# When a tile's transposing transfer and its merge are asked for in the last group of a decoder layer's first up-projection

## The chip, the cores and the metric

The kernel runs on one core of one Trainium2 chip. The metric is the device time of one execution in microseconds (us); lower is better. All inputs and outputs are float32.

## What is computed

The reference is one decoder layer over 256 positions of width 2048: a conditioned SwiGLU feed-forward part, a gated pair of token mixers, a second SwiGLU part and a final norm. The change lies in the first feed-forward part, `x + 0.5 * gate * SwiGLU1(h)`:

```
mod = (c_act @ w_ada[l] + b_ada[l]).reshape(b, N_MOD, D_MODEL)
h = modulate(rms_norm(x, norm_ffn1[l]), mod[:, 0], mod[:, 1])
x = x + 0.5 * mod[:, 2][:, None, :] * swiglu(h, w_ffn1_gu[l], w_ffn1_down[l])
...
def swiglu(h, w_gu, w_down):
    gate, up = jnp.split(h @ w_gu, 2, axis=-1)
    return (jax.nn.silu(gate) * up) @ w_down
```

`w_gu` is 2048 x 11264 and `w_down` 5632 x 2048. The product of silu(gate) and up has positions on its rows; the down-projection needs it turned, with positions on its columns.

## The kernel before

**Products.** Every product of full width is made of three: weights and activations are split in a high part (rounded to fp32r) and the rest, and `products` (L354 to L369) issues high x high, low x high and high x low on TensorE, for each of two tiles of 128 positions. A load of weights, 1 MB, goes through SP's DMA queue into one of four `raw` buffers. ScalarE casts it to the high part `wh` in two halves (L375), VectorE makes the rest `wl` (L377), and each half feeds 12 matmuls of 128x512. The pool of `wh` and `wl` has three buffers, so ScalarE can be almost three halves ahead of TensorE.

**The first up-projection.** Its first 16 half chunks of 512 columns (n = 0 to 15; even n a gate, odd n an up) are worked in four groups of the contraction, so that work can start before the whole of h is there. The loop stands at L1233. In the last group (`final`) each of the 16 visits takes one load of four blocks, so 24 matmuls. A visit n runs `visit` (its matmuls), then `ready` (the load of the next visit, and the cast of that load's first half), then `turn_step`, and behind an odd n `swiglu_up`, which adds the sums of the earlier groups, takes silu(gate) x up for the two tiles and leaves them to be turned. In this group only, `swiglu_up` is given `behind` (the last cast), so that silu comes behind it on ScalarE. Visits 0 to 7 also do passes of the conditioning (`tick`), which load rows of `w_ada` into the same four `raw` buffers.

**Turning a tile.** For n = 1, 3, 5, 7, 9 and 11 the two tiles are turned by DMA, in three steps each (L525): `apart` copies the tile into two planes of 16-bit words (ScalarE, two copies at L535, into one of three `flat` buffers); `turn` issues a transposing transfer on SP (L540) from `flat` to one of four `back` buffers; `together` merges the planes at the tile's place (ScalarE, two copies at L551). For n = 13 and 15 TensorE turns the tiles (L518). The lines that decide what a step waits for:

```
flat = ctx.enter_context(tc.tile_pool(name="flat", bufs=3))
back = ctx.enter_context(tc.tile_pool(name="back", bufs=4))
...
            with tc.issue_after(cast[-1]):
                for i in range(2):
                    nc.scalar.copy(planes[:, i, :], words(src)[:, :, i])
...
            turned = back.tile([P, 2, KB, P], U16, tag="back", name=nm("back"))
            nc.sync.dma_start_transpose(
...
            with tc.issue_after(cast[-1]):
                for i in range(2):
                    nc.scalar.copy(into[:, :, :, i], held["turned"][:, i])
```

**What sets the order.** SP's order is that of the program (`manual_schedule`, L103): an instruction that waits on SP holds all behind it. On the other engines a scheduler sets the order when the kernel is built; `issue_after(cast[-1])` keeps the copies of a step behind the latest cast that was issued when the step was reached. Since `ready` comes before `turn_step` in a visit, that is the cast of the first half of the next visit's load. `later` (L651) is the list of steps that a chunk's two tiles take, one a visit: in it, `a0, a1` are the plane copies of the two tiles, `t0, t1` the transposing transfers and `m0, m1` the merges. A chunk that ends at visit n does a0 at n+2, a1 at n+3, t0 at n+7, t1 at n+8 and both merges at n+10, so what n = 7 to 11 leave goes on among the gemm parts of `ffn_up` (L722), which follows the group and whose `turn_step` is at L444.

Of the kernel before, what the change touches and what calls it, by code (L numbers as in the profile page):

```python
# [77 lines left out]
def layer_kernel(  # L78
# [42 lines left out]
    def nm(s):  # L121
        uid[0] += 1
        return f"{s}_{uid[0]}"
# [10 lines left out]
    def t512():  # L134
        return tmp.tile([P, CH], F32, tag="t512", name=nm("t"))
# [188 lines left out]
    turns = []  # L324
# [189 lines left out]
    def transpose_to(dest, src_of, n, ps=None):  # L514

        ps = ps or bank()
        for j in range(n):
            nc.tensor.transpose(ps[:, j * P : (j + 1) * P], src_of(j), ident)  # L518
        nc.any.tensor_copy(dest, ps[:, : n * P])
# [5 lines left out]
    def turn_by_dma(dest, src, pool=flat, tag="flat"):  # L525


        held = {}

        def apart():  # L530
            planes = pool.tile([P, CH], F32, tag=tag, name=nm("flat"))
            planes = planes.bitcast(U16).rearrange("p (i n) -> p i n", i=2)
# [3 lines that stand above are left out]
            held["planes"] = planes  # L536

        def turn():
            turned = back.tile([P, 2, KB, P], U16, tag="back", name=nm("back"))
            nc.sync.dma_start_transpose(  # L540
                turned.rearrange("p i k n -> p (i k) n"),
                held["planes"].rearrange("p i n -> p (i n)"),
            )
            held["turned"] = turned

        into = dest.bitcast(U16).rearrange("p k (s i) -> p k s i", i=2)

        def together():
# [4 lines that stand above are left out]
        return apart, turn, together  # L553
# [97 lines left out]
    def later(work, then=None, quick=False):  # L651

        (a0, t0, m0), (a1, t1, m1) = work
        order = [a0, a1, None, None, None, t0, t1, None, m0]
        for f in order[:7] + order[7 + quick :]:
            yield
            if f is not None:
                f()
        m1()
        if then is not None:  # L660
            then()

    def later_by_pairs(work):

        for apart, _, _ in work:
            apart()
        for _ in range(5):
            yield
        for a in range(0, len(work), 2):
            for which in (1, 2):  # L670
                yield
                for parts in work[a : a + 2]:
                    parts[which]()
# [21 lines left out]
    def swiglu_up(banks_g, banks_u, tiles, ci, parts=None, by_dma=False, behind=None):  # L695

        k0 = ci * KB
        dest = tiles[k0 // KD].rearrange("p (k s) -> p k s", s=S)
        kk = k0 % KD
        work = []  # L700
        for t in range(NT):
            s = t512()
            g, u = banks_g[t], banks_u[t]
            if parts is not None:
                nc.vector.tensor_add(s, g, parts[0][t])
                nc.vector.tensor_add(parts[1][t], u, parts[1][t])
                g, u = s, parts[1][t]
            with nullcontext() if behind is None else tc.issue_after(behind):
                nc.scalar.activation(s, g, AF.Silu)
            nc.vector.tensor_mul(s, s, u)  # L710
            if by_dma:
                work.append(turn_by_dma(dest[:, kk : kk + KB, t * P : (t + 1) * P], s))
                continue
            transpose_to(
                dest[:, kk : kk + KB, t * P : (t + 1) * P],
                lambda j: s[:, j * P : (j + 1) * P],
                KB,
            )
        if work:
            turns.append(later(work))  # L720

    def ffn_up(held, w, tiles, first, bg=None, turned=(), ahead=None):  # L722
        for ci in range(first, DFF // CH):
            bg = bg or gemm(held, w, [ci * CH])[0]
            bu = gemm(held, w, [DFF + ci * CH], ahead=ahead)[0]
            swiglu_up(bg, bu, tiles, ci, by_dma=ci in turned)
            bg = ahead = None
# [240 lines left out]
    behind = [[back.tile([P, CH], F32, tag="back", name=nm("back")) for _ in range(NT)] for _ in range(2)]  # L968
# [264 lines left out]
    for g, ks in enumerate(groups):  # L1233
# [11 lines left out]
        for i, n in enumerate(order):  # L1245
# [31 lines left out]
            if not final:  # L1277
                to_parts(n)
            elif n % 2:
                swiglu_up(  # L1280
                    banks.pop(n - 1),
                    banks.pop(n),
                    tiles,
                    n // 2,
                    (part_of(n - 1), part_of(n)),
                    n // 2 < 6,
                    cast[-1],
                )
# [40 lines left out]
    work = []  # L1329
# [153 lines left out]
    for ci in range(4):  # L1483
        b = in_chunk(O_SQ + ci * CH)
        work = []
# [16 lines left out]
    for a, off in ((0, O_RQ), (1, O_RK)):  # L1502
        for ci in range(2):
            b = in_chunk(off + ci * CH)
            work = []
# [93 lines left out]
    for ci in range(4):  # L1599
        b = in_chunk(O_RG + ci * CH)  # L1600
        work = []
# [11 lines left out]
    for p in range(2):  # L1613
        sg = first if p == 0 else gates(p)
        c0s = [(2 * p + i) * CH for i in range(2)]
        for g, a, w in ((1, a_swa, w_swa_branch), (0, a_ret, w_ret_branch)):
            assert g == 1 or not turns
            banks = gemm(a, w[0], c0s)
            for i in range(2):
                for t in range(NT):  # L1620
                    nc.vector.tensor_mul(sg[:, g, i, t, :], sg[:, g, i, t, :], banks[i][t])
        work = []
        for i in range(2):
            for t in range(NT):
                m = sg[:, 0, i, t, :]
                nc.vector.tensor_add(m, m, sg[:, 1, i, t, :])
                k0 = (2 * p + i) * KB
                dest = mt[:, k0 : k0 + KB, t * P : (t + 1) * P]
                if p == 0 or i == 1:
                    work.append(turn_by_dma(dest, m, tmp, "t512"))  # L1630
                    continue
                transpose_to(dest, lambda j: m[:, j * P : (j + 1) * P], KB)
        soon(later_by_pairs(work) if p == 0 else later_at_once(work))
# [135 lines left out]
```

## Time and profile before

| what | before |
|---|---|
| median of 3 runs | 2367.28 us |
| the three runs | 2367.73, 2367.28, 2357.96 us |
| the profiled execution's own time | 2357.64 us |
| its span, from first to last instruction | 2355.5 us |
| mean granted TensorE clock | 0.999 |
| TensorE busy | 2335.7 us, 99% |
| VectorE busy | 1673.1 us, 71% |
| ScalarE busy | 1367.2 us, 58% |
| the last group of the first up-projection | about 289 to 377 us of the span |

Profiled times count from the start of the span. The profiled execution's own time holds 2.14 us more than the span, which lie around it. A DMA's row on SP is the time in which SP issues it; its landing is told apart, from issue to the last byte. Where a row says x2 or x4, its time runs from the first of them to the end of the last.

### The profile page before, as it was taken

Reading aid. Unit: us, or ns where it says so; the run is one execution under the profiler, and the core shown is the slowest. Engines: PE = TensorE matmul, PEld = TensorE weight load, DVE = VectorE, ACT = ScalarE, POOL = GpSimd, SP = SyncE. Lnnn points to the kernel's source line nnn. Section 1 sums busy time; section 2 is a strip of 40 time slices with the busy share of each in tenths; the row PEclk is TensorE's granted clock in tenths of the full one; section 3 lists DMA queues with packets and bytes.
Section 4 is the critical chain, followed back from the end, with each engine's and each line's share of the span. In section 5 each row is a group of like instructions: output and inputs, shape, how many; then the busy total and the mean of one; then the engine's idle time right before and its main releaser. Section 6 shows DMA issues by size and latency. Waiting matters only on the chain.

```text
span 2355.5 us, 28357 instructions
## 1 busy us (share of the span) xinstructions
PE 2335.7 (99%) x10445; PEld 1918.6 (81%) x10445; DVE 1673.1 (71%) x2576; ACT 1367.2 (58%) x1888; POOL 18.3 (1%) x27
## 2 busy tenths in 40 slices
PE   8999999999999999999999999999999999999998
PEld 5888888888888888778888888888888888888887
DVE  7788888778867768976777776676555555555656
ACT  6766567455556567774556564465455454455544
POOL 0000000000000000000000000000000000000000
PEclk9999999999999999999999999999999999999999
DMA  9989889988765889876778787754767768666553
GB/s 383 375 323 361 355 294 328 336 306 293 302 237 220 293 267 255 258 212 254 267 273 306 288 310 281 272 204 179 259 237 256 242 239 268 223 231 202 193 197 125
DMA packets 191901, 630.24 MB, mean 268 GB/s; under 512 B 113105, under 2 KB 114769, under 8 KB 121233
## 3 DMA queue, kind: packets, MB, share of 16 engines
q1 hardware_dynamic: 189266, 617.41, 74.6%
q0 software_dynamic: 1600, 9.83, 1.0%
q8 instruction: 82, 1.34, 0.2%
q10 hardware_dynamic: 896, 1.19, 0.1%
q14 instruction: 57, 0.47, 0.1%
HBM read 598.47 MB, written 4.22 MB: 256 GB/s over the span
## 4 chain that ended last, share of the span: by engine, by line
PE 96%; DMA 2%; DVE 1%; ACT 1%; issue 0%; SPq 0%; DVEq 0%; ACTq 0%
PE pa L360 93%; DMA raw<-in_w_ffn_gu_dram 1%; DMA rows_x<-in_w_ada_dram 1%; PE ps L1453 0%; DVE slot L220 0%; PE pd L1369 0%; DVE wl L377 0%; ACT wh L375 0%; DMA x_sb<-in_x_dram 0%; PE ps L360 0%; PE pa L1099 0%; PE ps L895 0%; PE pd L1099 0%; DVE rows_x L220 0%; PE ps L1369 0%
## 5 line engine op out<-in xcount | busy, mean ns | idle before, releaser
L377 DVE TENSOR_TENSOR wl<-raw,wh 128x1024 fp32r<-128x1024 f32 x792 | 963.5, 1225 | 511.0 <-ACT wh L375 451.6
L375 ACT CAST wh<-raw 128x1024 fp32r<-128x1024 f32 x792 | 830.6, 1054 | 818.7 <-PE pa L360 752.6
L360 PE MATMUL pa<-wh,hh 128*128 128x512 f32 x2184 | 597.0, 391 | 3.0 <-ACT wh L375 1.7
L360 PE MATMUL pa<-wh,hl 128*128 128x512 f32 x2184 | 592.6, 389 | 0.0
L360 PE MATMUL pa<-wl,hh 128*128 128x512 f32 x2184 | 586.2, 390 | 0.2
L360 PEld LDWEIGHTS pa<-wh,hh 128*128 128x128 f32 x2184 | 407.5, 188 | 91.6 <-ACT wh L375 2.9
L360 PEld LDWEIGHTS pa<-wl,hh 128*128 128x128 f32 x2184 | 409.4, 188 | 86.7 <-DVE wl L377 1.0
L360 PEld LDWEIGHTS pa<-wh,hl 128*128 128x128 f32 x2184 | 409.8, 188 | 86.1 <-issue 0.4
L360 PE MATMUL pa<-wh,a 128*128 128x512 f32 x1824 | 452.1, 389 | 0.0
L360 PEld LDWEIGHTS pa<-wh,a 128*128 128x128 f32 x1824 | 341.7, 188 | 70.6
L360 PE MATMUL pa<-wl,a 128*128 128x512 f32 x912 | 245.1, 389 | 0.0
L220 DVE CUSTOM_DVE_ANT_0 slot<-slot,cact 128x512 f32<-128x512 f32 (+2 forms) x288 | 219.3, 812 | 30.0 <-DMA slot<-in_w_ada_dram 29.5
L360 PEld LDWEIGHTS pa<-wl,a 128*128 128x128 f32 x912 | 171.1, 188 | 35.4
L551 ACT COPY slot<-back 128x512 uint16<-128x512 uint16 x148 | 98.7, 766 | 0.0
L220 DVE CUSTOM_DVE_ANT_0 rows_x<-rows_x,cact 128x512 f32<-128x512 f32 x124 | 78.7, 686 | 18.0 <-DMA rows_x<-in_w_ada_dram 17.8
L410 ACT CAST a<-slot 128x512 fp32r<-128x512 f32 x114 | 70.6, 620 | 29.3 <-PE pa L360 29.0
L535 ACT COPY flat<-t 128x512 uint16<-128x512 uint16 x136 | 76.7, 617 | 8.9 <-DVE t L1526 5.7
L411 DVE TENSOR_TENSOR a<-slot,a 128x512 fp32r<-128x512 f32 x114 | 77.8, 684 | 0.3 <-ACT a L410 0.3
L220 DVE CUSTOM_DVE_ANT_0 raw<-raw,cact 128x512 f32<-128x512 f32 (+1 forms) x92 | 60.7, 709 | 14.6 <-DMA raw<-in_w_ada_dram 14.5
L1219 ACT COPY slot<-pa 128x512 f32<-128x512 f32 x72 | 38.6, 589 | 21.2 <-PE pa L360 21.0
L360 PE MATMUL pa<-wh,home 128*128 128x512 f32 x160 | 39.5, 389 | 0.0
L220 DVE DVE_READ_ACCUMULATOR2_ANT sums<- 128x1 f32 x440 | 35.9, 82 | 0.0
(232 smaller groups left out, 1087.0 us busy)
## 6 DMA issues: line engine op xcount, KB each, us to landing
raw<-in_w_ffn_gu_dram SPq DMA_DIRECT2D x160, 1024.0 KB, 5.5
raw<-in_w_in_dram SPq DMA_DIRECT2D x104, 1024.0 KB, 5.8
raw<-in_w_ffn_down_dram SPq DMA_DIRECT2D x88, 1024.0 KB, 4.9
slot<-in_w_ada_dram SPq DMA_DIRECT2D x87, 1024.0 KB, 7.4
rows_x<-in_w_ada_dram SPq DMA_DIRECT2D x31, 1024.0 KB, 7.1
raw<-in_w_ada_dram SPq DMA_DIRECT2D x22, 1024.0 KB, 5.7
raw<-in_w_swa_branch_dram SPq DMA_DIRECT2D x16, 1024.0 KB, 5.0
raw<-in_w_ret_branch_dram SPq DMA_DIRECT2D x16, 1024.0 KB, 5.4
```

Source lines behind the costliest of these rows:

```text
L220: nc.vector.tensor_tensor_reduce(out=w[:, at], in0=w[:, at], in1=cact[:, at], scale=1.0, scalar=0.0, op0=ALU.mult, op1=ALU.add, accum_out= ...
L360: product = nc.tensor.matmul(banks[t], act[:, j, t * P : (t + 1) * P], weights[:, j, :], start=starts and i == 0 and j == 0, stop=ends and ...
L375: cast.append(nc.scalar.copy(hi, src).ins)
L377: low.append(nc.vector.tensor_sub(lo, src, hi.bitcast(F32)).ins)
L410: nc.scalar.copy(hi, v)
L411: nc.vector.tensor_sub(lo, v, hi.bitcast(F32))
L535: nc.scalar.copy(planes[:, i, :], words(src)[:, :, i])
L551: nc.scalar.copy(into[:, :, :, i], held["turned"][:, i])
L1219: nc.scalar.copy(p, b)
```

## The change

In the last group, and only there, the list `later` gives way to a new one, `evenly`. With it a chunk that ends at visit n does a0 at n+2, t0 and a1 at n+3, t1 at n+4, m0 at n+7 and m1 at n+8. The number of copies and transfers is the same. The list that the chunks of `ffn_up` take stays `later`.

```diff
+    def evenly(work):
+
+        (a0, t0, m0), (a1, t1, m1) = work
+        for fs in ((), (a0,), (t0, a1), (t1,), (), (), (m0,), (m1,)):
+            for f in fs:
+                f()
+            yield
+
...
         if work:
-            turns.append(later(work))
+            turns.append((later if behind is None else evenly)(work))
```

The new function moves every later line number up by eight (L1158 is L1166, L709 is L717).

SP's queue before, in the second half of the group. A transfer names its `back` buffer and its `flat` source; a load names its `raw` buffer; 484, 493, 504, 513, 524, 533 and 546 are the loads of visits 9 to 15, and 565 the first of `ffn_up`. These rows begin behind the load of visit 9:

```order
L540 DMA_TRANSPOSE back_487_2754<-flat_437_2510 128x8x128
L1158 DMA raw_493_2789<-in_w_ffn1_gu_dram 128x2048
L540 DMA_TRANSPOSE back_496_2795<-flat_447_2561 128x8x128
L1158 DMA raw_504_2840<-in_w_ffn1_gu_dram 128x2048
L540 DMA_TRANSPOSE back_507_2846<-flat_456_2604 128x8x128
L1158 DMA raw_513_2881<-in_w_ffn1_gu_dram 128x2048
L540 DMA_TRANSPOSE back_516_2891<-flat_466_2655 128x8x128
L1158 DMA raw_524_2936<-in_w_ffn1_gu_dram 128x2048
L540 DMA_TRANSPOSE back_527_2942<-flat_477_2705 128x8x128
L1158 DMA raw_533_2977<-in_w_ffn1_gu_dram 128x2048
```

The same place now, from the load of visit 9 (488) on; 497, 508, 517, 528, 537 and 550 are the loads of visits 10 to 15:

```order
L1166 DMA raw_488_2756<-in_w_ffn1_gu_dram 128x2048
L540 DMA_TRANSPOSE back_491_2764<-flat_481_2713 128x8x128
L1166 DMA raw_497_2799<-in_w_ffn1_gu_dram 128x2048
L540 DMA_TRANSPOSE back_500_2807<-flat_492_2766 128x8x128
L1166 DMA raw_508_2852<-in_w_ffn1_gu_dram 128x2048
L540 DMA_TRANSPOSE back_511_2860<-flat_501_2809 128x8x128
L1166 DMA raw_517_2895<-in_w_ffn1_gu_dram 128x2048
L540 DMA_TRANSPOSE back_520_2903<-flat_512_2862 128x8x128
L1166 DMA raw_528_2948<-in_w_ffn1_gu_dram 128x2048
```

Before, the transfer behind the load of visit 9 is the first of the twelve; now it is the fifth, and the first four (`back_447`, `back_457`, `back_468` and `back_480`) stand behind the loads of visits 5 to 8. From the fifth on a transfer takes a `back` buffer that an earlier one had, four before it.

ScalarE before, from the cast of the first half of the load of visit 12 (513) on. The two merges free the buffers `back_487` and `back_496`, which the transfers `back_527` and `back_536` take again:

```order
L375 CAST wh_514_2883<-raw_513_2881 128x1024
L551 COPY slot_8_117<-back_487_2754 128x4x128 x2
L551 COPY slot_8_117<-back_496_2795 128x4x128 x2
L709 ACTIVATE t_518_2896<-t_518_2896 128x512
L709 ACTIVATE t_519_2901<-t_519_2901 128x512
L375 CAST wh_522_2920<-raw_513_2881 128x1024
L535 COPY flat_508_2848<-t_479_2713 128x512 x2
L375 CAST wh_525_2938<-raw_524_2936 128x1024
```

ScalarE now, from the cast of the first half of the load of visit 9 (488) on; the merges free `back_447`, `back_457` and `back_468`, which the transfers `back_491`, `back_500` and `back_511` take again:

```order
L375 CAST wh_489_2758<-raw_488_2756 128x1024
L551 COPY slot_8_117<-back_447_2561 128x4x128 x2
L535 COPY flat_492_2766<-t_460_2616 128x512 x2
L375 CAST wh_495_2783<-raw_488_2756 128x1024
L375 CAST wh_498_2801<-raw_497_2799 128x1024
L551 COPY slot_8_117<-back_457_2606 128x4x128 x2
L535 COPY flat_501_2809<-t_482_2716 128x512 x2
L717 ACTIVATE t_502_2812<-t_502_2812 128x512
L717 ACTIVATE t_503_2817<-t_503_2817 128x512
L375 CAST wh_506_2836<-raw_497_2799 128x1024
L375 CAST wh_509_2854<-raw_508_2852 128x1024
L551 COPY slot_8_117<-back_468_2659 128x4x128 x2
```

Before, two tiles were merged at every second visit; now one tile is merged at each, directly behind the first cast of a load.

## The prediction, made before the changed kernel had run

> **What bounds the kernel now.** I read the page first, for the engine that carries the span.
>
> ```profile
> span 2355.5 us, 28357 instructions
> PE 2335.7 (99%) x10445; PEld 1918.6 (81%) x10445; DVE 1673.1 (71%) x2576; ACT 1367.2 (58%) x1888; POOL 18.3 (1%) x27
> PE 96%; DMA 2%; DVE 1%; ACT 1%; issue 0%; SPq 0%; DVEq 0%; ACTq 0%
> ```
>
> TensorE (PE) is busy for 99% of the span and makes 96% of the chain that ended last. Next I read the table of stretches over the last group; its columns are the busy time (and count) of PE, PEld, DVE, ACT and POOL, the granted clock, the DMA share and GB/s.
>
> ```profile
> 299.70:321.50 21.80, 21.80 (x98) 18.06 (x97) 21.66 (x38) 14.67 (x20) 0.00 (x0) 1.00 0.78 298
> 321.50:343.20 21.70, 21.70 (x98) 17.86 (x97) 18.94 (x29) 13.71 (x20) 2.16 (x4) 1.00 1.07 327
> 343.20:365.00 21.80, 21.80 (x98) 18.06 (x97) 15.58 (x19) 17.90 (x26) 0.00 (x0) 1.00 0.67 190
> ```
>
> TensorE has no idle time in any of them: 98 matmuls in 21.8 us, or 0.222 us each, so a visit's 24 take 5.3 us. Nothing in this group can give time back. What the change can do is to make TensorE wait where it doesn't now, and a matmul that comes late there is not made up for later, since the engine is full on both sides.
>
> So the question is how early the weights are. In ScalarE's order of time (start, duration, engine, line), these rows are the first cast of the load of visit 9, and of the load after visit 15, which is the first of `ffn_up`:
>
> ```profile
> 331.83 1.05 ACT L375 CAST wh<-raw 128x1024 fp32r<-128x1024 f32 x1 [1.19 <-issue]
> 371.56 1.04 ACT L375 CAST wh<-raw 128x1024 fp32r<-128x1024 f32 x1
> ```
>
> and in TensorE's order the transposes that stand behind six matmuls of visit 15, and the first four matmuls of the visit after it:
>
> ```profile
> 371.94 0.60 PE L518 MATMUL ps<-small_c,t 128*128 128x128 f32 x4
> 376.93 1.07 PE L360 MATMUL pa<-wh,hh 128*128 128x512 f32 x4
> ```
>
> TensorE uses that weight 5.4 us after its cast began (376.93 - 371.56). A cast takes 1.05, so some 4.3 us is all the cover there is.
>
> Last I read what SP, which asks for the weights in the program's order, waits for. First the longest row of SP's waits in the stretch 290 to 400, then SP's order of time:
>
> ```profile
> SPq L540 <- ACT slot L551: 34.0, 4, 13.1
> ...
> 338.20 0.33 SPq L1158 DMA_DIRECT2D raw<-in_w_ffn_gu_dram  x1
> 350.48 1.23 SPq L540 DMA_TRANSPOSE back<-flat  x1
> 351.81 0.53 SPq L1158 DMA_DIRECT2D raw<-in_w_ffn_gu_dram  x1
> 352.43 1.23 SPq L540 DMA_TRANSPOSE back<-flat  x1
> 353.76 0.74 SPq L1158 DMA_DIRECT2D raw<-in_w_ffn_gu_dram  x1
> ```
>
> This is the stall on which all turns. The transfer at 350.48 is `back_527`, the first that takes a `back` buffer again. SP waited for the merge that frees it (longest 13.1 us), and the load behind it went out only at 351.81. A transfer that waits holds the weights. Before, TensorE survives it, because the merge it waits for stands behind the cast of visit 12's load while the load it holds is that of visit 14: the load of visit 13 was out already, at 338.20, and two transfers are freed at once.
>
> **The change part by part.** The counts stay: twelve transfers, 24 plane copies and 24 merge copies. Two of the copies at L519 move from ScalarE to VectorE; both have idle time there, so they cost nothing.
>
> *The first four transfers* move up by four visits, into buffers that are free. They wait for plane copies now. A plane copy stands behind the first cast of a load, and the transfer holds the load two visits on; a round is cast, copy, transfer, load and landing, some 9 us by the rows below (0.96 + 1.04 + 1.33 + 5.6), against 10.7 for two visits. It just fits, and I cost it at nothing; what it may take off the cover of 4.3 us is in the upper bound.
>
> *The fifth transfer and those behind it* cost the time. By the orders shown, `back_491` needs the buffer of `back_447`, whose merge stands behind the first cast of visit 9's load (488); behind `back_491` on SP stands the load of visit 10 (497). Then `back_500` needs a merge behind the first cast of that very load, and holds the load of visit 11, and so on to the load after visit 15. From here on each load can be asked for only when the load before it has landed and been cast: a round is now one visit, not two.
>
> The round's pieces, from ScalarE's order of time, with the rows of SP above:
>
> ```profile
> 348.10 1.06 ACT L375 CAST wh<-raw 128x1024 fp32r<-128x1024 f32 x1 [1.14 <-PE pa L360]
> 349.06 2.66 ACT L551 COPY slot<-back 128x512 uint16<-128x512 uint16 x4
> 351.58 1.15 ACT L709 ACTIVATE t<-t 128x512 f32<-128x512 f32 x2
> ...
> 367.05 1.13 ACT L535 COPY flat<-t 128x512 uint16<-128x512 uint16 x2
> 368.09 1.05 ACT L375 CAST wh<-raw 128x1024 fp32r<-128x1024 f32 x1
> 369.04 2.66 ACT L551 COPY slot<-back 128x512 uint16<-128x512 uint16 x4
> ```
>
> Cast to merge is 0.96 us (348.10 to 349.06), merge to transfer 1.42 (349.06 to 350.48), transfer to load 1.33 (350.48 to 351.81): together 3.71. Then the load lands, and the next cast begins. Landings, from the DMA issues (count, KB, us to landing), alone in the stretches 351.7 to 352, 364.4 to 364.6 and 338.1 to 338.4, then the min, median and max of all loads of L351 and of L1158:
>
> ```profile
> raw<-in_w_ffn_gu_dram SPq DMA_DIRECT2D x1, 1024.0 KB, 5.6
> raw<-in_w_ffn_gu_dram SPq DMA_DIRECT2D x1, 1024.0 KB, 5.2
> raw<-in_w_ffn_gu_dram SPq DMA_DIRECT2D x1, 1024.0 KB, 9.2
> ...
> DMA to landing us min/median/max: 4.6/5.0/14.1
> ...
> DMA to landing us min/median/max: 4.9/7.8/14.2
> ```
>
> The first two went out right behind a transfer, with little else in flight, as the loads of the round would: I take 5.6. The third shared the engines with the gate row and constants that GpSimd loads at that time; the load of visit 10 meets these too, so it gets 7.4, half way from 5.6 to 9.2. From landing to cast I allow 0.1.
>
> The sum runs from the cast of visit 9, which I leave at 331.83, to that of the load after visit 15, seven loads on. Six steps of 3.71 make 22.3. The seventh is longer, for two transfers stand ahead of that load, and the second waits for the merge behind the *second* cast of visit 15: cast 0.96, merge pair 1.26 (half of 349.06 to 351.58), plane copies 1.04 (367.05 to 368.09), cast 0.95, merge to transfer 1.42, transfer to load 1.33, together 7.0. Landings: 7.4 + 6 x 5.6 = 41.0, and 7 x 0.1 = 0.7. In all 22.3 + 7.0 + 41.0 + 0.7 = 71.0, so the cast begins at 402.8 and TensorE can use it at 403.9, a cast of 1.05 later. Now it does at 376.93. The loss is 27.0 us; it includes the use of the cover, which is gone after the first round or two.
>
> Bounds: with every landing at 4.6, the smallest, the landings are 32.2 and the loss 18; with every one at the median of 7.8, 54.6 and 41. Below that lies only a failure of the mechanism (a rival).
>
> Against: the silent gain. The four waits of SP, 34.0 us in all, change their place and are worth nothing where they are, as TensorE had no idle time in 299.7 to 365.
>
> Here a rule of the Trainium skill speaks differently. Its page "DMA: Bandwidth & Descriptors", section "Issuing engines are not separate DMA queues", says that who starts a DMA matters only for the issuing sequencer's time, which is usually small beside the transfer. By that the twelve transfers would cost their issue alone wherever they stand, and the sum would be zero. SP's 13.1 us ahead of 350.48 disagree: the time of the sequencer here is its wait, not its issue.
>
> On the profiled execution's own time, 2357.64 us (span 2355.5 and 2.14 around it), 27.0 make 2384.6. The runs of before lie at two levels, about 2358 (one run, and the profile) and 2367.5 (two runs, with the median of 2367.28), and no view tells me why. On the upper level it would be 2394.5. I predict the middle, 2389.
>
> **The rivals.**
>
> *The weights stay hidden (not slower).* The loads asked for ahead of the fifth transfer would carry TensorE to the end of the round. From 331.83 to 375.88, the latest start of a cast that keeps 376.93, there are 44.05 us; the issue parts and the small lags take 22.3 + 7.0 + 0.7 = 30.0, which leaves 14.05 for seven landings, 2.0 each. Hidden means landings of 2.0 us or less. The smallest row says 4.6. It could still be so if a merge came ahead of the cast. Time: as before, 2357.6 to 2367.5. Chance 0.07.
>
> *Early asking pays (not slower either).* A transfer that is asked four visits earlier has landed long before its merge, so ScalarE never waits for it and the merge comes sooner; SP would then wait less, and more loads would be ahead. For it is this row, of those who wait for the transfers in the group:
>
> ```profile
>   ACT flat L535: 2.5, 3
> ```
>
> Three times ScalarE waits 2.5 us in all for a transfer to free its `flat` buffer, and that would go. Against it: a merge is placed by the step list, not by the landing, and no wait is ended by a landing in the round above. Gain at most nothing, for want of idle time on TensorE: 2357.6 to 2367.5. Chance 0.05.
>
> The Trainium skill's page "DMA: Bandwidth & Descriptors", section "Rules for kernel authors", is of this mind: issue a DMA early, wait for it late, and its fixed cost overlaps. What it leaves open is what stands behind the early one in the same queue.
>
> *Congestion (slower still).* If the transfers' issue takes long again and the landings are long, the round grows.
>
> ```profile
> L540 SPq DMA_TRANSPOSE back<-flat x12: 1231/1234/2640, 321.8 to 383.3; - x12
> ```
>
> These are the min, median and max in ns of a transfer's issue in the group. With 2.64 in place of 1.23 for the seven issues of the sum (+9.9) and seven landings of 7.8 (54.6 in place of 41.0, +13.6) the loss is 50.5: 2408 to 2418. Against it: in the round only one load and one transfer are in flight at a time, and the rows of `w_ada` come only before visit 8. Chance 0.06.
>
> **How the numbers follow.** The forecast has 0.82; its own range, 18 to 41 us on either level, is 2375.6 to 2408.5. The two hidden cases have 0.12 and lie below 2370, congestion 0.06 above; leaving both out is within the 2 in 10, so the range is 2374 to 2407. About 0.5%, or 12 us, is what a measurement of this kernel can tell from no change. Faster by more than that has no mechanism, only the spread of the runs: 0.02. Within: the two hidden cases, 0.10 of them, and 0.03 for the low end of the forecast against an upper level of before: 0.13. Slower: 0.85.
>
> **What would show it.** In the profile after: TensorE idle in visits 10 to 15, and none before 340; its idle time ended by ScalarE's cast (L375), and the casts waiting for DMA of `raw`; SP's loads of visits 11 to 15 about 9.4 us apart, each 1.3 us behind a transfer; SP's wait for the merges (L551) in most of eight places; and from the second load of `ffn_up` on the same rate as before. The prediction is wrong if loads there go out every 5.3 us, if the gaps on TensorE are ended by something else than the casts, or if a loss of this size stands outside 340 to 405.

## The result and the profile after

| what | before | after |
|---|---|---|
| median, executions beside each other (6 and 6) | 2361.03 us | 2385.89 us |
| lowest and highest of them | 2356.32 to 2367.73 us | 2383.84 to 2387.37 us |
| the profiled execution's own time | 2357.64 us | 2386.35 us |
| its span | 2355.5 us | 2384.2 us |
| TensorE takes the first weights of `ffn_up` | 376.93 us | 404.46 us |

The kernel is slower: ratio 1.0101, 95% interval 1.0081 to 1.0121. Before lies mostly between 2355.5 and 2360 us and now and then between 2363 and 2368.5, and its six executions here hold both, so their median lies in between; in the two sets run beside the experiments its medians are 2356.92 (25 executions) and 2357.32 (17). Against these two medians, and between the two profiled executions, the loss is 28.6 to 29.0 us.

The page of after: the span, the busy time by engine, the shares of the chain that ended last, and the group of matmuls whose idle time grew (busy us, mean ns, idle us just before them and what ended most of it).

```profile
span 2384.2 us, 28354 instructions
PE 2346.1 (98%) x10445; PEld 1922.6 (81%) x10445; DVE 1675.6 (70%) x2578; ACT 1366.2 (57%) x1886; POOL 18.6 (1%) x27
PE 93%; DMA 3%; DVE 2%; ACT 1%; issue 1%; SPq 0%; DVEq 0%; ACTq 0%
L360 PE MATMUL pa<-wh,hh 128*128 128x512 f32 x2184 | 600.0, 393 | 18.4 <-ACT wh L375 17.6
```

The work is the same and TensorE still has nearly all of the chain. What moved is the idle time of one group of matmuls, 18.4 us, ended by the casts; before it was this row:

```profile
L360 PE MATMUL pa<-wh,hh 128*128 128x512 f32 x2184 | 597.0, 391 | 3.0 <-ACT wh L375 1.7
```

Where it lies shows in the table of stretches of after (the same columns as in the prediction):

```profile
321.50:343.20 21.70, 21.50 (x96) 17.35 (x94) 16.22 (x26) 10.63 (x16) 2.17 (x4) 1.00 0.91 249
343.20:365.00 21.80, 14.12 (x50) 10.13 (x51) 10.53 (x13) 11.27 (x17) 0.00 (x0) 0.92 0.48 145
365.00:387.00 22.00, 17.60 (x64) 13.26 (x62) 10.69 (x13) 13.16 (x21) 0.00 (x0) 0.85 0.52 137
387.00:409.00 22.00, 15.39 (x61) 11.37 (x60) 14.55 (x23) 13.01 (x20) 0.00 (x0) 0.85 0.69 244
409.00:431.00 22.00, 22.00 (x98) 18.21 (x97) 15.24 (x27) 13.91 (x18) 0.00 (x0) 1.00 0.98 400
```

In three stretches TensorE does 50, 64 and 61 matmuls where 21.8 us held 98 before; to 342.6 and from 409 on it is full. The DMA share falls to about a half in the middle: the transfer engines are idle half of the time just when weights are wanted. That speaks against a lack of bandwidth. The chain of waits, cut to 290 to 420, says what the time went to instead: first its head line for before, then for after pieces of it (start, duration, what), the load of visit 8, then those from the load of visit 10 on, with one round in full, and the end.

```profile
by line: PE pa L360 98.8%; PE ps L518 1.3%; PE ps L295 0.1%
```

```profile
319.72 9.79 DMA raw<-in_w_ffn_gu_dram
...
337.35 7.78 DMA raw<-in_w_ffn_gu_dram
345.23 0.37 ACT wh L375
345.83 0.36 issue
346.18 1.41 ACT slot L551 x2
347.59 1.00 ACT flat L535 x2
348.95 5.30 DMA raw<-in_w_ffn_gu_dram
...
358.06 5.20 DMA raw<-in_w_ffn_gu_dram
...
390.81 0.85 ACT wh L375
...
397.73 5.54 DMA raw<-in_w_ffn_gu_dram
403.37 1.05 ACT wh L375
404.46 15.59 PE pa L360 x58
```

The chain has no piece of TensorE from 310 to 404. From the load of visit 10 on it goes in a circle: a load, a cast, a merge, a transfer, and the next load. (At 347.59 it names plane copies, L535, where SP's order has a transfer at 347.62; more on this name below.) SP's order of time shows the circle from its side:

```profile
335.95 1.29 SPq L540 DMA_TRANSPOSE back<-flat  x1
337.35 0.52 SPq L1166 DMA_DIRECT2D raw<-in_w_ffn_gu_dram  x1
347.62 1.24 SPq L540 DMA_TRANSPOSE back<-flat  x1
348.95 0.53 SPq L1166 DMA_DIRECT2D raw<-in_w_ffn_gu_dram  x1
...
358.06 0.53 SPq L1166 DMA_DIRECT2D raw<-in_w_ffn_gu_dram  x1
...
393.19 4.48 SPq L540 DMA_TRANSPOSE back<-flat  x2
397.73 0.57 SPq L351 DMA_DIRECT2D raw<-in_w_ffn_gu_dram  x1
```

Each load of these rounds goes out 1.33 to 1.47 us behind the start of a transfer, about 0.1 behind the end of its issue, and loads are 9.1 us apart (348.95 to 358.06) where a visit's matmuls last 5.3. Last, who waits in 290 to 412 (total us, times, longest), and rows of ScalarE, the plane copy of visit 8 and then one round:

```profile
SPq L540 <- ACT flat L535: 72.5, 9, 10.9
...
PEld pa L360 <- ACT wh L375: 20.1, 10, 3.7
```

```profile
335.79 1.13 ACT L535 COPY flat<-t 128x512 uint16<-128x512 uint16 x2
...
345.23 1.04 ACT L375 CAST wh<-raw 128x1024 fp32r<-128x1024 f32 x1 [7.36 <-DMA raw<-in_w_ffn_gu_dram]
346.18 1.41 ACT L551 COPY slot<-back 128x512 uint16<-128x512 uint16 x2
347.45 1.12 ACT L535 COPY flat<-t 128x512 uint16<-128x512 uint16 x2
```

The profile puts SP's 72.5 us down to the plane copies (L535), not to the merges (L551). The rows speak for the merge: its pair ends at 347.59 (346.18 + 1.41), the transfer starts at 347.62, and the plane copies end only at 348.57, so the transfer didn't wait for them. Nor did it wait for the planes that it reads itself, `flat_492`: by ScalarE's order these were copied at 335.79 and were ready at 336.92, more than 10 us earlier. Merge and plane copies stand next to each other on ScalarE, and the name is inferred. The experiments decide between merge and plane copy in another way.

### The profile page after: what moved, and what is told of

It is laid out like the page before. It is cut to its first block, busy times and chain, and to the rows that moved or that the text cites. A ratio compares the mean times of both kernels' runs of the same rounds, so it can differ in the third digit from the quotient of the medians.

```text
span 2384.2 us, 28354 instructions
## 1 busy us (share of the span) xinstructions
PE 2346.1 (98%) x10445; PEld 1922.6 (81%) x10445; DVE 1675.6 (70%) x2578; ACT 1366.2 (57%) x1886; POOL 18.6 (1%) x27
## 4 chain that ended last, share of the span: by engine, by line
PE 93%; DMA 3%; DVE 2%; ACT 1%; issue 1%; SPq 0%; DVEq 0%; ACTq 0%
PE pa L360 91%; DMA raw<-in_w_ffn_gu_dram 2%; DVE slot L220 1%; PE ps L1461 0%; DVE wl L377 0%; ACT wh L375 0%; ACT slot L551 0%; PE pd L1377 0%; DMA x_sb<-in_x_dram 0%; ACT flat L535 0%; DVE raw L220 0%; PE ps L360 0%; PE pa L1107 0%; PE ps L903 0%; PE pd L1107 0%
## 5 line engine op out<-in xcount | busy, mean ns | idle before, releaser
L360 PE MATMUL pa<-wh,hh 128*128 128x512 f32 x2184 | 600.0, 393 | 18.4 <-ACT wh L375 17.6
L551 ACT COPY slot<-back 128x512 uint16<-128x512 uint16 x148 | 99.6, 767 | 0.0
L535 ACT COPY flat<-t 128x512 uint16<-128x512 uint16 x136 | 76.7, 617 | 6.3 <-DVE t L1534 5.3
```

The costliest lines, as they stand in the source:

```text
L360: product = nc.tensor.matmul(banks[t], act[:, j, t * P : (t + 1) * P], weights[:, j, :], start=starts and i == 0 and j == 0, stop=ends and ...
```

## The experiments

The theories, by the letters of the texts on record. **A**, the prediction's: a transfer waits for a merge, to have one of four `back` buffers again, and holds the next load; the round then costs 9 us a visit. **B**: the transfer waits for a plane copy, as the profile names it. **C**: the earlier transfers slow the DMA engines themselves. **D**: a price paid once, not by the round. **E**: the price arises only at the end of the group, where two transfers stand ahead of one load.

### More buffers for the turned tiles

The third and the sixth chunk of the group put their turned tiles in the unused end of the row tile; everything is asked for where the change asks for it, but a transfer no longer meets a merge of the round before.

```diff
-            turned = back.tile([P, 2, KB, P], U16, tag="back", name=nm("back"))
+            turned = home or back.tile([P, 2, KB, P], U16, tag="back", name=nm("back"))
...
+                home = more_back[t] if behind is not None and ci % 3 == 2 else None
...
+        whole_row = one.tile([P, D], F32, tag="row", name="root_row")
+        root_row.append(whole_row[:, :S])
+        for i in range(2):
+            more_back.append(
+                whole_row[:, S + i * CH : S + (i + 1) * CH]
+                .bitcast(U16)
+                .rearrange("p (i k n) -> p i k n", i=2, k=KB)
+            )
```

> The changed kernel with two more buffers for turned tiles: the transfers of every third chunk of the group (n = 5 and 11) land in the unused end of the row tile, so a transfer takes a buffer again only after six. Theory A (buffers: the fifth and later transfers wait on SP for a merge behind the cast of the load just ahead, and hold the next load): the merge that a transfer needs is now two visits older, SP isn't held, loss 0 to 4 us of the 25, so 2361 to 2365 us where before takes 2361, and loads of visits 11 to 15 again some 5.4 us apart. Theory B (planes: the transfer waits for the plane copy that stands one visit ahead of it, which the profile names as the one waited for): the buffers don't matter, 2383 to 2388. Theory C (the earlier transfers slow the loads on the DMA engines): 2383 to 2388.

Measured: median 2356.43 us beside 2356.92 of before, ratio 0.9993 (0.9979 to 1.0007). The whole loss is gone. SP's order of time in this kernel, and its stretch from 343:

```profile
341.18 1.24 SPq L540 DMA_TRANSPOSE back<-flat  x1
342.51 0.53 SPq L1178 DMA_DIRECT2D raw<-in_w_ffn_gu_dram  x1
346.45 1.24 SPq L540 DMA_TRANSPOSE back<-flat  x1
347.78 0.53 SPq L1178 DMA_DIRECT2D raw<-in_w_ffn_gu_dram  x1
```

```profile
343.20:365.00 21.80, 21.80 (x98) 18.06 (x97) 18.14 (x22) 20.33 (x30) 0.00 (x0) 1.00 0.88 245
```

The transfers stand in the same places of the queue, one ahead of each load, but loads go out 5.3 us apart (342.51 to 347.78). A stands. B falls, since a transfer's plane copy is where it was; so does C, since the twelve early transfers still run.

### The merges a visit sooner, and the transfers a visit later

Two kernels leave the buffers alone and change only the list, so that a visit lies between a merge and the transfer that needs its buffer.

```diff
-        for fs in ((), (a0,), (t0, a1), (t1,), (), (), (m0,), (m1,)):
+        for fs in ((), (a0,), (t0, a1), (t1,), (), (m0,), (m1,)):
```

> The changed kernel with both merges one visit sooner (one empty visit fewer in the list), all transfers where the change has them. Theory A: the fifth transfer's merge now stands behind the cast of a load two ahead of the load it holds; a round of 9.1 us is spread over two visits of 5.3 to 5.4, 10.7 in all, so the loss is 0 to 5 us: 2361 to 2366. Theory B: the plane copies stand as they do, 2383 to 2388. Theory C: 2383 to 2388.

```diff
-        for fs in ((), (a0,), (t0, a1), (t1,), (), (), (m0,), (m1,)):
+        for fs in ((), (a0,), (a1,), (t0,), (t1,), (), (m0,), (m1,)):
```

> The changed kernel with both transfers one visit later (two visits behind the plane copy), merges where the change has them. Theory A: a transfer that needs a merge stands one load further back, the round is again two visits long, loss 0 to 5 us: 2361 to 2366. Theory B: the plane copy has one visit more, loss also gone, 2361 to 2366. Theory C: nearly as many transfers run beside the same loads, 2380 to 2388.

Measured: merges sooner 2359.67 us, ratio 0.9999 (0.9984 to 1.0015); transfers later 2356.81, ratio 0.9997 (0.9988 to 1.0007). Each gives the loss back, the first but for a rest: its executions, 2358.83 to 2361.97, have a median 2.75 us above that of before beside them, and its profiled span is 1.3 us longer (2356.8). With the merges sooner TensorE still shows a short hole, the 1.27 us that it lacks in the first of these rows; the second is the same stretch with the transfers later:

```profile
343.20:365.00 21.80, 20.53 (x89) 16.32 (x89) 17.38 (x21) 21.19 (x33) 0.00 (x0) 1.00 0.89 260
```

```profile
343.20:365.00 21.80, 21.80 (x98) 18.06 (x97) 16.20 (x20) 20.15 (x30) 0.00 (x0) 1.00 0.89 253
```

So a round of two visits does fit, and only just; the second list has no such hole. It moves the transfers by one visit each, and the loss is gone: against C once more. The second list doesn't part A from B, and was not meant to; the first does, since its plane copies stay where they were.

### The merges freed from the casts

The merges of this group need no longer stand behind the latest cast; the scheduler may put them where they fit.

```diff
-            with tc.issue_after(cast[-1]):
+            with nullcontext() if free else tc.issue_after(cast[-1]):
                 for i in range(2):
                     nc.scalar.copy(into[:, :, :, i], held["turned"][:, i])
...
+                        dest[:, kk : kk + KB, t * P : (t + 1) * P], s, free=behind is not None
```

> The changed kernel without the rule that keeps a merge behind the latest cast, in this group alone; the scheduler then puts each merge about one visit behind its transfer, so every buffer is free long before it is taken again. SP's order is that of the change. Theory A: no transfer waits for a merge, no load is held: 2357 to 2362. If ScalarE, whose casts stand behind the merges, waits for the transfers' landings instead (a transfer landed in 3 to 12 us before): up to 10 us more, 2362 to 2370. Theories by which the transfers' place alone costs the time: 2380 to 2385.

Measured: 2358.1 us, ratio 0.9999 (0.9988 to 1.001). A short hole is left on TensorE, 1.41 us of the stretch from 365:

```profile
365.00:387.00 22.00, 20.59 (x95) 16.72 (x94) 17.22 (x27) 14.32 (x20) 0.00 (x0) 1.00 0.76 289
```

Here the link from the cast to the merge is cut, with the buffers, the list and the queue as in the change, and the loss is gone. One link is cut by no run alone: that on SP a waiting transfer holds the next load. It is seen in the rows, where a load goes out 0.1 us behind the transfer's issue each time.

### The new list for four of the six chunks

```diff
-            turns.append((later if behind is None else evenly)(work))
+            turns.append((later if behind is None or ci > 3 else evenly)(work))
```

> The changed kernel with the new list for the first four chunks of the group (n = 1 to 7) and the old one for n = 9 and 11, so that four transfers, not eight, wait for a merge just ahead and hold a load (those of visits 10 to 13); the loads of visits 14 and 15 and the first of ffn_up are free. Theory A (a price by the round): in the changed kernel the cast of visit 13 stood at 372.5, TensorE would start it at 373.6, where before it starts at 359.7: a loss of 14 us, 2371 where before takes 2357. Rival D (a price paid once, by the gate row's traffic at the first long landing and the lower clock behind it): nearly the whole loss, 22 to 27 us, 2379 to 2384. Rival E (the end: two transfers ahead of the first load of ffn_up): 0 to 4 us, 2357 to 2361.

Measured: 2371.53 us beside 2357.32, ratio 1.0056 (1.0043 to 1.0069): 14.2 us, half of the loss. SP's order of time, in its last two rounds:

```profile
355.87 1.23 SPq L540 DMA_TRANSPOSE back<-flat  x1
357.19 0.53 SPq L1166 DMA_DIRECT2D raw<-in_w_ffn_gu_dram  x1
364.87 1.23 SPq L540 DMA_TRANSPOSE back<-flat  x1
366.20 1.49 SPq L1166 DMA_DIRECT2D raw<-in_w_ffn_gu_dram  x3
```

The last round takes 9.0 us (355.87 to 364.87), as in the change, and at the fourth held load they stop: no transfer stands behind it, so three loads go out at once. Four held loads cost half of what seven cost, so the price is by the round. D (2379 to 2384) and E (2357 to 2361) fall.

### The transfers on ScalarE's queue

If a waiting transfer costs because of what stands behind it on SP, it should be free on another queue.

```diff
-            nc.sync.dma_start_transpose(
+            queue.dma_start_transpose(
...
+                queue = nc.sync if behind is None else nc.scalar
```

> The changed kernel with the group's twelve transfers issued by ScalarE instead of SP, the steps as in the change. Theory A: the transfers still wait for the same merges, which now stand ahead of them on the same engine, and no load stands behind them on SP; the loss is what twelve issues of 1.2 us do to ScalarE's casts, 0 to 6 us: 2361 to 2367. Theory B: the same, 2361 to 2367. Theory C: the same transfers run on the same DMA engines at the same times, 2380 to 2388.

Measured: 2398.54 us, ratio 1.0168 (1.0143 to 1.0194): a miss for every theory, and slower than the change. On SP no transfer stood ahead of a load any more (first row: six loads in one piece, from 318 to 363). They still went out late: by SP's waits of 290 to 420 they waited for VectorE's use of the weights loaded earlier (second row), which comes behind the casts. And in ScalarE's order of time the issues of two transfers stand as long rows:

```profile
318.03 44.87 SPq L1169 DMA_DIRECT2D raw<-in_w_ffn_gu_dram  x6
```

```profile
SPq L1169 <- DVE wl L377: 51.2, 9, 12.8
```

```profile
326.81 11.65 ACTq L540 DMA_TRANSPOSE back<-flat  x1
349.85 10.01 ACTq L540 DMA_TRANSPOSE back<-flat  x1
```

and in the waits of 290 to 420 TensorE waits up to 9.9 us for a cast, where the longest in the change was 3.7:

```profile
PEld pa L360 <- ACT wh L375: 32.0, 5, 9.9
```

The expectation's price, twelve issues of 1.2 us, was wrong: four of the twelve took 3.56 to 11.65 us, and on ScalarE the casts stand behind them. While ScalarE issues a transfer for 11.65 us (326.81 to 338.46) it casts nothing. The run therefore says nothing for or against A. Why an issue took up to 11.65 us there, where on SP it took 1.23 to 2.64 before, was not tried further and stays open.

## Why the prediction was right

It said 2389 us with a range of 2374 to 2407 and a chance of 0.85 for slower; it came to 2385.89. Step by step:

**What bounds the kernel.** Right: TensorE was full, and what it now waits for can't be made up; from 409 on it runs 98 matmuls in 22.0 us again.

**The first four transfers, costed at nothing.** Nearly. There is no gap on TensorE ahead of 342.6, but some cover went. These casts stand at the start, for the loads of visits 8 and 9:

```profile
329.59 1.05 ACT L375 CAST wh<-raw 128x1024 fp32r<-128x1024 f32 x1 [2.65 <-DMA raw<-in_w_ffn_gu_dram]
...
333.59 1.04 ACT L375 CAST wh<-raw 128x1024 fp32r<-128x1024 f32 x1
```

The load of visit 8 went out at 319.72 and took 9.79 us in the chain, where before it went out from 317.79 on and took some 5.6; the cast of visit 9 began at 333.59 and not at 331.83. These 1.8 us the sum lacked. What made that load late was not tried; in the kernel with more buffers it goes out as late, at 319.31, and TensorE doesn't wait.

**The round from the fifth transfer on.** Right in each piece. Cast to merge is 0.95 (forecast 0.96), merge to transfer 1.44 (1.42), transfer to load 1.33 (1.33). From the cast at 345.23 (of visit 10's load) to that at 390.81 (of visit 15's) there are five rounds, 9.1 each; forecast 9.4, since the landings took 5.2 to 5.4 where 5.6 stood in the sum. The first, long one took 7.78 (7.4).

**The last step, 7.0.** It took 6.92, from the cast at 390.81 to the load at 397.73, with both transfers ahead of that load in the row at 393.19.

**The sum.** From 333.59 to 403.37 are 69.8 us, forecast 71.0. The later start (1.8 longer) and the rest of the sum (1.2 shorter) cancel to 0.6 us, which is luck: the cast was forecast for 402.8, TensorE for 403.9, and it came at 404.46.

**A term that the sum lacks.** Of the 28.7 us between the profiled spans 27.5 lie ahead of that matmul. The other 1.2 are, all but some 0.2, the sum of two things. The first twelve matmuls of `ffn_up` took 5.00 us and not 2.7, at half the clock (2.3 us more; the rows are in the last section). And the eight transposes of the tiles of n = 15, which before stood behind this point (384.86), were done ahead of it, in a wait (400.60); that gives back some 0.9. The sum had neither.

**What would show it.** Right except for one line, the name of SP's wait: it carries the name of the plane copies and not of the merges; the kernel with more buffers shows that the buffers decide all the same. One reading was a little off: the rows leave SP 11.95 us of waiting ahead of 350.48 (338.20 + 0.33 to 350.48), not 13.1; no term of the sum uses it.

**The level.** The prediction took the middle of two levels of before, for want of a view that tells them apart. All six executions of after, 2383.84 to 2387.37, lie near 2384.6, the forecast for the lower one. So the 3.1 us between the forecast of 2389 and the median are the 4.4 of this choice, less the 1.3 by which the median lies above 2384.6. The range did not depend on the choice.

**The rivals.** Hidden weights needed landings of 2.0 us; the smallest in the round was 5.18. That early asking pays is answered by the kernel with more buffers: there the transfers are early, no load is held, and it gains nothing measurable (0.9993). Congestion didn't come: the DMA share fell to 0.48.

**The rule against it.** In the kernel with more buffers the twelve early transfers cost nothing measurable. That is as the Trainium skill's page "DMA: Bandwidth & Descriptors", section "Issuing engines are not separate DMA queues", has it: who starts a DMA matters only for the sequencer's time. The rule doesn't speak of a DMA that waits, and the change shows that one: with the transfers in the same places but waiting for their buffers, 1.0101. Its remark that this time is usually small beside the DMA fits most of the issues on ScalarE (median 1.78 us, landing 15.5), but not the two of 11.65 and 10.01 us.

## What to carry to other kernels

Asking for a transfer earlier cost nothing by itself here; what it waits for, and what stands behind it in the same queue, sets the price, so follow a reused buffer back to the instruction that frees it. If that instruction is placed behind the arrival of a load, and the waiting transfer holds the next load, the loads run one at a time, at landing plus all the steps between, and the price is that less what TensorE needs, for each round, once the cover is used up. Two more buffers, one visit more between merge and transfer, or a merge not tied to the cast each broke the circle; none of them was faster than the kernel before, in which TensorE had no idle time to give.

## What the runs showed of the hardware

**TensorE at a lower clock where it waits, and just behind.** In the three stretches with gaps the granted clock is 0.92, 0.85 and 0.85, and 1.00 before and after. A matmul there takes 0.282 us (14.12 / 50), 0.275 and 0.252, against 0.222 in a full stretch. Summed over those 175 matmuls that is 8.3 us more (47.11 - 175 x 0.222), so it stands as busy time and not as idle: TensorE's busy time grew by 10.4 us (2346.1 - 2335.7) with the same 10445 matmuls, and its idle time, the rest of the span, by 18.3 (38.1 - 19.8). A reader who counts only the idle time finds two thirds of the loss.

Within the rounds the clock did not set the pace, for the next load was waited for anyway. Behind the last wait it did. These are a stretch there, with its granted clock of 0.50, and TensorE's first and fourth rows (start, duration) from that matmul on:

```profile
404.50:409.00 4.50, 4.50 (x11) 3.57 (x12) 4.50 (x9) 2.84 (x4) 0.00 (x0) 0.50 1.01 428
```

```profile
404.46 2.08 PE L360 MATMUL pa<-wh,hh 128*128 128x512 f32 x4 [2.63 <-ACT wh L375]
...
409.46 1.07 PE L360 MATMUL pa<-wh,hh 128*128 128x512 f32 x4
```

From 404.46 to 409.46, with the weights there, twelve matmuls take 5.00 us, where twelve of 0.222 take 2.7: 2.3 us of the loss. The Trainium skill's page "TensorE: Matmul & The Clock Gate", section "Part 1: The HAM clock gate", says that a monitor sets the clock by how busy the array was lately; these rows agree with it in direction.

**Some issues of a transfer took long on ScalarE.** These rows give count, then min, median and max in ns of the twelve issues when ScalarE makes them, and their landing in 307 to 412 of that kernel (count, median us):

```profile
L540 ACTq DMA_TRANSPOSE back<-flat x12: 1248/1784/11646, 307.5 to 411.7; - x12
```

```profile
back<-flat ACTq DMA_TRANSPOSE x12, 15.5
```

On SP the slowest of twelve took 2.64 us before. With both queues at work the transfers landed after 15.5 us (6.1 in the group before) and the loads of that stretch after 12.5 (7.8 was the median of all loads of L1158 before). That would fit DMA engines shared by more at a time; that this made the issue long is a guess.
